# Halving a group's last hidden chunk earlier, finishing only the sums a norm needs, and GpSimd's low halves in two instructions, in a two-block fp32 network

## The chip, the cores and the metric

One NeuronCore of a Trainium2 chip runs the whole network in one launch. The metric is the device time of one execution in microseconds (us); lower is better. The kernel is bound to one core, so its own span is the time, but for some 2 us around it.

## The reference, cut to what matters

Two blocks run one after the other on 256 tokens of width 1024, all in fp32. The first block has two layers with a 256-token context stream beside the latent one; every norm in it is modulated by a vector (shift, scale, gate) that is itself a product of a conditioning vector with a 1024 x 6144 matrix.

```python
mod = split(silu(c) @ w_mod[i] + b_mod[i], 6)          # sh1, sc1, ga1, sh2, sc2, ga2
...
h = rmsnorm(x, g_pre_mix) * (1 + sc1) + sh1
u = h @ w_in                                            # four mixers, then w_out
...
x = x + ga1 * rmsnorm(y, g_post_mix)
hm = rmsnorm(x, g_pre_mlp) * (1 + sc2) + sh2
x = x + ga2 * rmsnorm(square(relu(hm @ w_mlp1)) @ w_mlp2, g_post_mlp)
```

In the first layer the context rows pass through the same MLP (hidden width 4096), so that MLP works on 512 tokens; this wide MLP is where the first part of the change lies. The second block is an attention block with a gated convolutional feed-forward of hidden width 2816.

## The kernel before, in words

**Three matmuls for one.** Every fp32 product is made of three float32r matmuls (`mm3`, lines 430 to 432): high by high, low by high, high by low. So every weight is split into a high half H (ACT, a copy that rounds) and a low half L (raw minus H).

**Weight units.** The weights come as a list of 128 x 1024 units in the order of their use. `fetch` brings two units (1 MB) per DMA from SP into one of four `raw` buffers. `step` splits the next unit: H by ACT (line 373), L by line 375, a subtraction of two SBUF operands, on DVE for 197 units and on POOL for 117, as the place in the program decides. Last-minute units are split in two halves of 512 columns into other buffers (`uH` line 366, `uL` line 367, POOL). Six H and six L buffers exist. `take(lead)` hands out the next unit and first sees to it that units up to `lead` places further on are split (`pump`): the lead thus sets where the H and L instructions stand in the program order of ACT and DVE.

**Modulation.** The list also holds units of the modulation matrix ("mod" units), spread over the program, two at a time. `mods` takes them: they aren't split; DVE (lines 692, 696), or ACT with POOL (lines 688, 690), scales each by the conditioning vector and adds it to an accumulator `macc`, 128 x 512, twice per unit. When a vector is whole, PE sums over partitions (`mod`, line 706), DVE adds the bias (`mr`, line 710) and, for a gate, the post-norm's gain (line 657); later steps that turn the row into columns (`modT`, PE line 770, DVE copy line 775) or into a split gate row (`mrh`, ACT lines 665 and 666, DVE line 667) are put in a list, `later`, and done where `run_later` is called.

**The wide MLP** (`mlp_wide`) has nine steps, g = 0 to 8. Step g makes four hidden chunks of 128 hidden rows by 512 tokens (`m1`, 24 matmuls of 512 columns for each, in one PSUM bank), then multiplies the four chunks of step g-1 with four `m2` units into 4 x 2 output tiles (96 matmuls), which DVE adds to `yacc`. `hidden` turns a chunk into its squared relu, split: ACT `rl` (line 1807) and `hidH` (1813), DVE `m` (1814) and `hidL` (1815), which is the last reader of the chunk's PSUM bank. Two mod units stand after chunk 1 and after chunk 3 of a step and two more pairs among the products. At chunk 3 the four m2 units are taken with leads 3, 2, 1, 0, and taking the first of them does the two mod units that stand ahead of it. The first output tile pair (`first[0]`, `first[1]`) is computed with chunks 0 to 2 first (9 matmuls each) and chunk 3 after. At g = 6 PE also makes the rows of a gate (`gaT`, line 812), which ACT (line 818) and DVE (line 816) copy out of PSUM as `ga`.

**From layer 0 to layer 1.** During step 8 the output tiles are finished row block by row block: post norm, `gp` (line 948), new `X` (line 962), statistics, `xn` (line 846). Then PE transposes `xn` (`hT`, line 886), DVE and ACT make `hF`, `hH`, `hL` (lines 870, 874, 875) with the modulation columns that `affine` hands out, and the first product of layer 1 (`ag`) starts. `affine` empties the whole `later` list first.

**Where GpSimd's subtractions stand.** Most of the 117 POOL subtractions come in bursts of 2 to 6 at the norms between stages, and three per step in the feed-forward at the end of the program (1345 to 1454 us).

Of the kernel before, what the change touches and what calls it, by code (L numbers as in the profile page):

```python
# [16 lines left out]
ALU = mybir.AluOpType  # L17
# [35 lines left out]
M1_MODS = ((0, 0, 0, 0), (0, 0, 0, 2), (0, 2, 0, 2), (0, 2, 0, 2)) + ((0, 2, 0, 2),) * 4  # L53
# [250 lines left out]
class Program:  # L304
# [45 lines left out]
    def step(self, pool=False, k2=False):  # L350

        nc = self.nc
        self.fetch()
        m = self.entries[self.next_entry][1]
        t = self.raw[self.next_entry]
        j = self.part
        self.n += 1
        if self.unit_names[len(self.units)][0] == "mod":
            self.units.append((t[:, j, :], self.next_entry))
            self.waiting[self.next_entry] = self.waiting.get(self.next_entry, 0) + 1  # L360
        elif k2:
            u = []
            for i in range(2):
                hi, lo = self.k2("uH", dt=F32R), self.k2("uL", dt=F32R)
                src = t[:, j, 512 * i:512 * i + 512]
                nc.scalar.activation(hi, src, AF.Copy)  # L366
                nc.gpsimd.tensor_tensor(lo, src, hi, op=ALU.subtract)  # L367
                u.append((hi, lo))
            self.units.append(u)
        else:  # L370
            hi = self.splitp.tile([128, 1024], F32R, tag="H", name=f"H_{self.n}")
            lo = self.splitp.tile([128, 1024], F32R, tag="L", name=f"L_{self.n}")
            nc.scalar.activation(hi, t[:, j, :], AF.Copy)  # L373
            pool = pool or (self.pool_l and len(self.units) % self.pool_l == 0)
            (nc.gpsimd if pool else nc.vector).tensor_tensor(lo, t[:, j, :], hi, op=ALU.subtract)  # L375
            self.units.append((hi, lo))
        self.part = (j + 1) % m
        t = None
        if self.part == 0:
            del self.raw[self.next_entry]  # L380
            if self.next_entry in self.waiting:
                self.held.add(self.next_entry)
            self.next_entry += 1
            self.fetch()

    def pump(self, upto, pool=(), k2=False):

        pool = list(pool)
        while len(self.units) <= upto and self.next_entry < len(self.entries):
            if len(self.units) > self.used and len(self.held) > RAW_BUFS - 2 and self.unit_names[len(self.units)][0] == "mod":  # L390
                break
            self.step(pool.pop(0) if pool else False, k2)
# [392 lines left out]

    def affine(self, l, which, i):

        self.run_later(True)
        return self.modT[l, 3 * which + 1][:, i], self.modT[l, 3 * which][:, i]

    def bcast_row(self, i, half):
# [1026 lines left out]
    def mlp_wide(self, l, hs, ctx_part, gates):  # L1818

        nc, v = self.nc, self.nc.vector  # L1820
        yacc, hids, h = {}, {}, hs[0]

        def product(ps, hid, us, t, hf, j):
            a = tuple(z[:, 128 * t:128 * t + 128] for z in hid[j])
            b = tuple(z[:, 512 * hf:512 * hf + 512] for z in us[j])
            self.mm3(ps, a, b, j == 0, j == 3)

        for g in range(9):
            if g < 8:
                hids.setdefault(g, [])  # L1830
                if g == 1:
                    self.pool_l = MLP_POOL
                if g == 0:
                    us = [self.unit("m1", lead=max(3 - j, 0)) for j in range(6)]
                    bk = [self.ps("m1") for _ in range(6)]
                    for j in range(0, 6, 2):
                        self.chunks(us[j:j + 2], h, 0, 256, bk[j:j + 2])
                    ctx_part(lambda k0: k0 and self.chunks(us[:2], h, 256, 512, bk[:2], range(k0 - 2, k0)))
                    self.chunks(us[:2], h, 256, 512, bk[:2], range(6, 8))
                    hids[1] = []  # L1840
                    for j in range(6):
                        if j > 1:
                            self.chunk(us[j], h, [(256, 512)], bk[j])
                        us[j] = None
                        self.hidden(bk[j], 512, hids[j // 4])
                        bk[j] = None
                        self.pump(self.used + j)
                else:
                    for j in range(len(hids[g]), 4):
                        ps = self.flat_chunk("m1", h, [(0, 512)])  # L1850
                        if j == 1 and g > 3:
                            self.mods(2, 0)
                        if j == 3:
                            us = [self.unit("m2", lead=3 - j) for j in range(4)]
                        self.hidden(ps, 512, hids[g])
            if g == 7:
                self.pool_l = False
                h = None
                hs.clear()
            if g == ROPE_AT[0]:  # L1860
                self.rope_tables()
            if g == ROPE_AT[1]:
                self.rope_rows()
                self.lam_value()
            if g == 6:
                gates()
            if g > 0:
                if g == 8:
                    us = [self.unit("m2", lead=3 - j) for j in range(4)]
                    self.pump(self.used + 1)  # L1870
                hid = hids.pop(g - 1)
                first = [self.ps("m2") for _ in range(2)] if g < 8 else ()
                for t in range(4):
                    for hf in range(2):
                        ps = first[hf] if t == 0 and first else self.ps("m2")
                        js = range(4)
                        if t == 0 and first:
                            js = (3,)
                            if hf == 0:
                                for i in range(2):  # L1880
                                    for j in range(3):
                                        product(first[i], hid, us, 0, i, j)
                        for j in js:
                            if g == 8 and t == 3 and hf == 1 and j == 2:
                                us[:2] = None, None
                                yield None
                            product(ps, hid, us, t, hf, j)
                        if hf and t == 0:
                            first = ()
                        if g < 8 and 2 * t + hf in M2_PUMP:  # L1890
                            self.pump(self.used + M2_PUMP[2 * t + hf] + (g == 7))
                        if g == 1:
                            yacc[t, hf] = self.k2("yacc")
                            nc.scalar.activation(yacc[t, hf], ps, AF.Copy)
                        elif g < 8:
                            v.tensor_tensor(yacc[t, hf], ps, yacc[t, hf], op=ALU.add)
                        if g < 8:
                            self.mods(M2_MODS[g][2 * t + hf], 0)
                        else:
                            yield ps, yacc.pop((t, hf))  # L1900

    def ffn_narrow(self, step, downs, name, nj, ga, xn=None):


# [7 lines left out]
        for i, ds in enumerate(downs):  # L1912
            if i == len(downs) - FFN_OFF:
                self.pool_l = False
            if xn is None and i == len(downs) - 1:
                self.pump(self.used + END_H)
                self.pump(self.used + 8, k2=True)
            hid.update(step(i))
            for c in ds:
                if not acc:  # L1920
                    acc = [[self.ps("acc") for _ in range(2)] for _ in range(2)]
                u = self.unit(name)
                for t in range(2):
                    for hf in range(2):
                        down(c, u, t, hf)
                u = None
                del hid[c]
# [24 lines left out]
    def block1(self, l, h):  # L1952
# [58 lines left out]
        for _ in self.ffn_narrow(step, MLP_DOWN, "m2", 32, ga, out):  # L2011
            h = None
            pairs += self.new_pairs()
            self.pre_tile(out[0], self.pk("pre_mix_2", 0, 8), None, pairs, 0)
# [509 lines left out]
```

## Time and profile before

| what | value |
|---|---|
| median of 3 runs (lowest to highest) | 1493.54 us (1491.67 to 1496.65) |
| the profiled execution's own time | 1495.41 us |
| its span, first to last instruction | 1493.2 us |
| busy: PE, PEld | 1428.6 us (96%), 1194.3 us |
| busy: DVE, ACT, POOL | 941.1, 768.4, 544.0 us |
| mean granted TensorE clock | 0.987 |

The busy shares are of the span. PE is busy nearly always, so what can be had is in PE's waits and in the stretches where its clock was granted at half. A row of the timeline shows the start, the length and, in brackets, the idle time just before and what ended it. A 512-column matmul is drawn 0.39 us long but the next one starts 0.22 to 0.23 us after it, since matmuls are pipelined.

### The profile page before, as it was taken

How to read it: one execution, taken by the hardware profiler on the slowest of the kernel's cores; microseconds unless marked ns; L12 is line 12 of the kernel's file. 1: busy time of each engine (PE TensorE's matmuls, PEld its weight loads, DVE VectorE, ACT ScalarE, POOL GpSimd, SP SyncE). 2: the span in 40 equal slices, each digit the busy share in tenths (PEclk: the TensorE clock that was granted, in tenths of full speed). 3: DMA queues.
4: the chain of work that ended last, by engine and by line, in shares of the span. 5: the costliest groups of instructions: out<-in, count | busy, mean ns of one | idle time of the engine just before them, and what ended most of it. 6: DMA issues, size and time to landing. Idle time of an engine off the chain costs nothing.

```text
span 1493.2 us, 21581 instructions
## 1 busy us (share of the span) xinstructions
PE 1428.6 (96%) x8260; PEld 1194.3 (80%) x8260; DVE 941.1 (63%) x1642; ACT 768.4 (51%) x1406; POOL 544.0 (36%) x351
## 2 busy tenths in 40 slices
PE   8989999999999998998899899998999999999998
PEld 7766767888778787877777689996888899789997
DVE  4685573765866676788776765556466666754335
ACT  4446564555553323345666554455434664556554
POOL 2384531203551500007263500005022555738882
PEclk9999999999999999998999999999999999999999
DMA  9653631124554553634242455555555433545551
GB/s 342 211 199 142 140 110 69 60 83 165 178 194 160 191 204 130 220 146 149 87 84 93 142 187 180 187 180 189 180 188 190 138 122 113 203 148 186 177 190 57
DMA packets 73103, 235.71 MB, mean 158 GB/s; under 512 B 13536, under 2 KB 14248, under 8 KB 73000
## 3 DMA queue, kind: packets, MB, share of 16 engines
q1 hardware_dynamic: 72280, 233.65, 46.3%
q8 instruction: 65, 1.06, 0.3%
q10 hardware_dynamic: 720, 0.69, 0.1%
q14 instruction: 38, 0.31, 0.1%
HBM read 233.27 MB, written 1.05 MB: 157 GB/s over the span
## 4 chain that ended last, share of the span: by engine, by line
PE 72%; DVE 16%; ACT 8%; issue 2%; DMA 1%; SPq 0%; DVEq 0%; ACTq 0%
PE m L431 8%; PE m L432 8%; PE m L430 8%; PE acc L430 3%; PE acc L431 3%; PE acc L432 3%; DVE L L375 3%; PE pj L431 2%; PE pj L430 2%; PE pj L432 2%; PE up L430 2%; PE up L432 2%; PE up L431 2%; ACT H L373 2%; ACT P L1447 1%
## 5 line engine op out<-in xcount | busy, mean ns | idle before, releaser
L375 POOL TENSOR_TENSOR L<-raw,H 128x1024 fp32r<-128x1024 f32 x117 | 283.3, 2443 | 323.0 <-ACT H L373 305.6
L373 ACT ACTIVATE H<-raw 128x1024 fp32r<-128x1024 f32 x314 | 317.3, 1050 | 131.4 <-PE m L432 48.1
L375 DVE TENSOR_TENSOR L<-raw,H 128x1024 fp32r<-128x1024 f32 x197 | 254.6, 1321 | 90.4 <-ACT H L373 87.8
L367 POOL TENSOR_TENSOR uL<-raw,uH 128x512 fp32r<-128x512 f32 x32 | 46.1, 1472 | 192.1 <-ACT uH L366 192.1
L431 PE MATMUL m<-hL,H 128*128 128x512 f32 (+1 forms) x304 | 109.0, 358 | 2.0 <-DVE hL L875 2.0
L430 PE MATMUL m<-hH,H 128*128 128x512 f32 (+1 forms) x304 | 109.0, 358 | 1.0 <-ACT hH L874 1.0
L432 PE MATMUL m<-hH,L 128*128 128x512 f32 (+1 forms) x304 | 108.7, 358 | 1.2 <-DVE L L375 1.2
L431 PE MATMUL m<-L,hidH 128*128 128x512 f32 x256 | 101.7, 397 | 4.2 <-DVE L L375 4.2
L1807 ACT ACTIVATE rl<-m 128x512 f32<-128x512 f32 (+1 forms) x56 | 28.3, 505 | 150.3 <-PE m L432 150.1
L430 PE MATMUL m<-H,hidH 128*128 128x512 f32 x256 | 101.7, 397 | 3.9 <-DVE hidL L1815 3.9
L432 PE MATMUL m<-H,hidL 128*128 128x512 f32 x256 | 100.7, 393 | 0.0
L690 POOL TENSOR_TENSOR macc<-mt,macc 128x512 f32<-128x512 f32 x42 | 61.1, 1494 | 92.3 <-ACT mt L688 92.3
L1026 POOL TENSOR_TENSOR cfacc<-cft,cfacc 128x512 f32<-128x512 f32 (+1 forms) x60 | 64.6, 1077 | 54.7 <-ACT cft L1025 50.8
L430 PE MATMUL up<-h,H 128*128 128x256 f32 x288 | 81.8, 284 | 0.0
L432 PE MATMUL up<-h,L 128*128 128x256 f32 x288 | 81.5, 283 | 0.0
L431 PE MATMUL up<-h,H 128*128 128x256 f32 x288 | 81.5, 283 | 0.0
L1814 DVE TENSOR_TENSOR m<-m,rl 128x512 f32<-128x512 f32 (+1 forms) x56 | 32.7, 584 | 76.6 <-ACT rl L1807 76.4
L696 DVE SCALAR_TENSOR_TENSOR macc<-raw,csil,macc 128x512 f32<-128x512 f32 x98 | 66.9, 749 | 0.0
L431 PEld LDWEIGHTS m<-hL,H 128*128 128x128 f32 x304 | 57.7, 190 | 10.9 <-DVE hL L875 2.6
L432 PEld LDWEIGHTS m<-hH,L 128*128 128x128 f32 x304 | 57.8, 190 | 10.1 <-DVE L L375 2.0
L430 PEld LDWEIGHTS m<-hH,H 128*128 128x128 f32 x304 | 57.9, 190 | 9.2 <-ACT hH L874 1.2
L2099 POOL TENSOR_TENSOR ra<-ra,rb 128x512 f32<-128x512 f32 x16 | 21.6, 1351 | 113.8 <-DVE rb L2097 113.3
(547 smaller groups left out, 4060.5 us busy)
## 6 DMA issues: line engine op xcount, KB each, us to landing
raw<-in_wst SPq DMA_DIRECT2D x208, 1024.0 KB
mod<-in_wmod SPq DMA_DIRECT2D x16, 256.0 KB
X<-in_x SPq DMA_DIRECT2D x4, 512.0 KB
nab<-in_rpb SPq DMA_DIRECT2D x32, 64.0 KB
raw<-in_wst SPq DMA_DIRECT2D x2, 512.0 KB
wuq<-in_small SPq DMA_DIRECT2D x4, 256.0 KB
cst<-in_c SPq DMA_DIRECT2D x4, 256.0 KB
grow<-in_rows SPq DMA_DIRECT2D x4, 256.0 KB
```

The lines of the kernel that those rows point to most:

```text
L367: nc.gpsimd.tensor_tensor(lo, src, hi, op=ALU.subtract)
L373: nc.scalar.activation(hi, t[:, j, :], AF.Copy)
L375: (nc.gpsimd if pool else nc.vector).tensor_tensor(lo, t[:, j, :], hi, op=ALU.subtract)
L430: mm(out, a[0], b[0], start=start, stop=False)
L431: mm(out, a[0], b[1], start=False, stop=False)
L432: mm(out, a[1], b[0], start=False, stop=stop)
L690: nc.gpsimd.tensor_tensor(o, t, o, op=ALU.add)
L696: v.scalar_tensor_tensor(acc[i][j], a, c, o, op0=ALU.mult, op1=ALU.add)
L1026: nc.gpsimd.tensor_tensor(acc, t, acc, op=ALU.add)
L1807: nc.scalar.activation(r[:, :T], ps[:, :T], AF.Relu)
L1814: v.tensor_tensor(ps[:, :T], ps[:, :T], r[:, :T], op=ALU.mult)
L2099: self.nc.gpsimd.tensor_tensor(a, a, b, op=ALU.add)
```

## The change

Three edits, and nothing else:

1. In `mlp_wide`, chunk 3 of a step is taken with a lead that reaches over the two mod units to the fourth m2 unit (4 + 2 = 6 places where two mod units follow, 4 where none does), so that all m2 units are split before the mod units are worked on; and `hidden` is called for a chunk right behind its matmuls, before the mod units instead of behind them.
2. `affine` does `later` steps only until the two column sets that it hands out exist; the rest is done at a new call in step 8 of the wide MLP, ahead of the products of the second row block, or where `run_later` is called next.
3. `low_half` makes the L of a unit: on POOL as two subtractions of 128 x 512, on DVE as one of 128 x 1024 as before. A reader of the first 512 columns waits for the first of the two alone.

```diff
@@ step
-            (nc.gpsimd if pool else nc.vector).tensor_tensor(lo, t[:, j, :], hi, op=ALU.subtract)
+            self.low_half(lo, t[:, j, :], hi, pool)
...
+    def low_half(self, lo, src, hi, pool):
+
+        e, n = (self.nc.gpsimd, 512) if pool else (self.nc.vector, 1024)
+        for o in range(0, 1024, n):
+            e.tensor_tensor(lo[:, o:o + n], src[:, o:o + n], hi[:, o:o + n], op=ALU.subtract)
...
@@ affine
-        self.run_later(True)
+        while any((l, 3 * which + j) not in self.modT for j in range(2)):
+            self.later.pop(0)[1]()
...
@@ mlp_wide
-                        ps = self.flat_chunk("m1", h, [(0, 512)])
+                        ps = self.flat_chunk("m1", h, [(0, 512)], 4 + M1_MODS[g][3] if j == 3 else None)
+                        self.hidden(ps, 512, hids[g])
                         if j == 1 and g > 3:
                             self.mods(2, 0)
                         if j == 3:
                             us = [self.unit("m2", lead=3 - j) for j in range(4)]
-                        self.hidden(ps, 512, hids[g])
...
+                        if g == 8 and t == 1 and hf == 0:
+                            self.run_later()
```

How the instructions move is seen best in the order of each engine. On DVE, at the end of step g = 6 of the wide MLP (L is the low half of a weight unit, `mr` a finished modulation row, `macc` the work on two mod units, `m` and `hidL` chunk 3's hidden values), it stood before:

```order
L375 TENSOR_TENSOR L_5240<-raw_5114,H_5239 128x1024
L710 TENSOR_TENSOR mr_4_5275<-mod_5270,brow 128x256
L375 TENSOR_TENSOR L_5278<-raw_5161,H_5277 128x1024
L692 TENSOR_SCALAR macc_5283<-raw_5077,csil 128x512
L692 TENSOR_SCALAR macc_5284<-raw_5077,csil 128x512
L375 TENSOR_TENSOR L_5288<-raw_5161,H_5287 128x1024
L696 SCALAR_TENSOR_TENSOR macc_5283<-raw_5077,csil,macc_5283 128x512
L696 SCALAR_TENSOR_TENSOR macc_5284<-raw_5077,csil,macc_5284 128x512
L1814 TENSOR_TENSOR m_1049_5245<-m_1049_5245,rl_5297 128x512
L1815 TENSOR_TENSOR hidL_5300<-m_1049_5245,hidH_5299 128x512
```

and with the change:

```order
L390 TENSOR_TENSOR L_5259<-raw_5133,H_5258 128x1024
L390 TENSOR_TENSOR L_5265<-raw_5180,H_5264 128x1024
L390 TENSOR_TENSOR L_5269<-raw_5180,H_5268 128x1024
L716 TENSOR_TENSOR mr_4_5304<-mod_5299,brow 128x256
L1821 TENSOR_TENSOR m_1052_5274<-m_1052_5274,rl_5306 128x512
L1822 TENSOR_TENSOR hidL_5309<-m_1052_5274,hidH_5308 128x512
L698 TENSOR_SCALAR macc_5315<-raw_5096,csil 128x512
L698 TENSOR_SCALAR macc_5316<-raw_5096,csil 128x512
L702 SCALAR_TENSOR_TENSOR macc_5315<-raw_5096,csil,macc_5315 128x512
L702 SCALAR_TENSOR_TENSOR macc_5316<-raw_5096,csil,macc_5316 128x512
```

Two L moved ahead of `mr`, and `m` and `hidL` ahead of four `macc`; the other steps from 2 on have the same pattern, on ACT the third H and `rl`, `hidH` move ahead of its own `macc` work likewise.

On PE, at the passage from layer 0 to layer 1 (m is the last output tile of the MLP, hT the transposes of layer 1's normalised rows), it stood before:

```order
L432 MATMUL m_1199_6024<-H_5800,hidL_5568 128x512
L770 MATMUL modT_6047<-ident,mr_3_5644 128x128 x2
L706 MATMUL mod_6053<-macc_5777,pick 32x256 x2
L706 MATMUL mod_6053<-macc_5779,pick 32x256 x2
L886 MATMUL hT_6065<-ident,xn_5906 128x128
```

and with the change the three rows stand some 66 matmuls earlier, at the start of the second row block's products:

```order
L438 MATMUL m_1157_5879<-H_5844,hidL_5678 128x512
L776 MATMUL modT_5930<-ident,mr_3_5673 128x128 x2
L712 MATMUL mod_5936<-macc_5796,pick 32x256 x2
L712 MATMUL mod_5936<-macc_5798,pick 32x256 x2
L436 MATMUL m_1173_5929<-H_5815,hidH_5540 128x512
```

Their DVE work (`modT` copies, `mr` twice) moves with them, and the DVE step `mrh` of the same vector moves from ahead of the first `hF` to later in layer 1.

On POOL the instructions keep their order; each L becomes a pair, here the first three (cfacc is the depthwise convolution), before:

```order
L375 TENSOR_TENSOR L_1474<-raw_1362,H_1473 128x1024
L1026 TENSOR_TENSOR cfacc_903<-cft_1488,cfacc_903 128x512
L1026 TENSOR_TENSOR cfacc_903<-cft_1491,cfacc_903 128x512
L1026 TENSOR_TENSOR cfacc_903<-cft_1494,cfacc_903 128x512
L375 TENSOR_TENSOR L_1552<-raw_1483,H_1551 128x1024
L375 TENSOR_TENSOR L_1562<-raw_1483,H_1561 128x1024
```

and with the change:

```order
L390 TENSOR_TENSOR L_1474<-raw_1362,H_1473 128x512 x2
L1033 TENSOR_TENSOR cfacc_903<-cft_1489,cfacc_903 128x512
L1033 TENSOR_TENSOR cfacc_903<-cft_1492,cfacc_903 128x512
L1033 TENSOR_TENSOR cfacc_903<-cft_1495,cfacc_903 128x512
L390 TENSOR_TENSOR L_1553<-raw_1484,H_1552 128x512 x2
L390 TENSOR_TENSOR L_1564<-raw_1484,H_1563 128x512 x2
```

Only the shape and the count of the L rows changed.

## Rows read from the trace of the kernel before

**Rows 1.** The page: busy time of each engine; the chain that ended last.

```profile
PE 1428.6 (96%) x8260; PEld 1194.3 (80%) x8260; DVE 941.1 (63%) x1642; ACT 768.4 (51%) x1406; POOL 544.0 (36%) x351
...
PE 72%; DVE 16%; ACT 8%; issue 2%; DMA 1%; SPq 0%; DVEq 0%; ACTq 0%
```

**Rows 2.** Waits of PE, whole span: waited for, us in total, times, longest.

```profile
PE m L431 <- DVE L L375: 4.2, 7, 1.6
PE ab L432 <- DVE h L912: 4.1, 5, 0.9
...
PE tok L431 <- POOL L L375: 2.5, 2, 1.8
```

**Rows 3.** Timeline of DVE, end of step 2's chunks.

```profile
383.26 0.42 DVE L710 TENSOR_TENSOR mr<-mod,brow 128x256 f32<-128x256 f32 x1 [2.45 <-PE mod L706]
...
384.20 2.30 DVE L375 TENSOR_TENSOR L<-raw,H 128x1024 fp32r<-128x1024 f32 x1
```

**Rows 4.** Waits of PE in 384 to 392, 430 to 438, 520 to 528.

```profile
PE m L431 <- DVE L L375: 2.1, 2, 1.6
...
PE m L431 <- DVE L L375: 0.7, 2, 0.5
...
PE m L431 <- DVE L L375: 0.3, 1, 0.3
```

**Rows 5.** Timeline of DVE, end of step 6's chunks.

```profile
567.83 0.42 DVE L710 TENSOR_TENSOR mr<-mod,brow 128x256 f32<-128x256 f32 x1 [2.57 <-PE mod L706]
568.16 1.22 DVE L375 TENSOR_TENSOR L<-raw,H 128x1024 fp32r<-128x1024 f32 x1
...
573.33 0.69 DVE L1814 TENSOR_TENSOR m<-m,rl 128x512 f32<-128x512 f32 x1
574.12 0.69 DVE L1815 TENSOR_TENSOR hidL<-m,hidH 128x512 fp32r<-128x512 f32 x1
```

**Rows 6.** Timeline of PE, first products of step 6.

```profile
570.37 0.39 PE L431 MATMUL m<-L,hidH 128*128 128x512 f32 x1
570.59 0.39 PE L432 MATMUL m<-H,hidL 128*128 128x512 f32 x1
574.87 0.79 PE L430 MATMUL m<-H,hidH 128*128 128x512 f32 x1 [3.89 <-DVE hidL L1815]
```

**Rows 7.** Windows: busy (instructions) by engine, PEclk, DMA share, GB/s.

```profile
574.00:580.00 6.00, 5.13 (x12) 4.07 (x13) 2.50 (x10) 3.18 (x5) 0.08 (x1) 0.50 0.86 334
```

**Rows 8.** Timeline of ACT, step 6.

```profile
562.96 2.94 ACT L373 ACTIVATE H<-raw 128x1024 fp32r<-128x1024 f32 x3
...
575.24 1.07 ACT L818 ACTIVATE ga<-gaT 128x512 f32<-128x512 f32 x2
```

**Rows 9.** Timeline of PE, passage from layer 0 to layer 1.

```profile
664.58 0.64 PE L706 MATMUL mod<-macc,pick 128*32 128x256 f32 x8
...
669.92 0.39 PE L430 MATMUL ag<-hH,H 128*128 128x256 f32 x1 [1.11 <-ACT hH L874]
```

**Rows 10.** Timeline of DVE, the same passage.

```profile
668.48 0.48 DVE L667 SCALAR_TENSOR_TENSOR mrh<-mrh,low,mr 128x256 fp32r<-128x256 f32 x1 [1.03 <-ACT mr L666]
```

**Rows 11.** Timeline of POOL: last feed-forward, last units, then three bursts at norms.

```profile
1394.37 7.15 POOL L375 TENSOR_TENSOR L<-raw,H 128x1024 fp32r<-128x1024 f32 x3 [1.35 <-ACT H L373]
...
1464.77 8.44 POOL L367 TENSOR_TENSOR uL<-raw,uH 128x512 fp32r<-128x512 f32 x6 [8.49 <-ACT uH L366]
...
284.00 4.90 POOL L375 TENSOR_TENSOR L<-raw,H 128x1024 fp32r<-128x1024 f32 x2 [30.42 <-ACT H L373]
...
835.46 10.16 POOL L375 TENSOR_TENSOR L<-raw,H 128x1024 fp32r<-128x1024 f32 x4
...
1345.22 14.23 POOL L375 TENSOR_TENSOR L<-raw,H 128x1024 fp32r<-128x1024 f32 x6 [4.16 <-ACT H L373]
```

**Rows 12.** DVE during the burst at 835; line 912: duration ns min/median/max.

```profile
838.56 4.81 DVE L912 TENSOR_TENSOR h<-hF,h 128x256 fp32r<-128x256 f32 x2
...
L912 DVE TENSOR_TENSOR h<-hF,h x24: 409/426/2602, 835.0 to 1311.0; 128x256 fp32r<-128x256 f32 x24
```

## The prediction

> **What bounds the kernel now.** I read the page first. PE is busy 96% of the span, and 72% of the chain of waits is PE [rows 1]; so a change that takes no matmul away can only win what PE waits for, and what its clock loses behind a wait. The waits of PE come next: a long list of short ones, of which three groups bear on the change, DVE's L (4.2 us), DVE's h (4.1) and POOL's L (2.5) [rows 2]; hidL stands apart, with one wait of 3.89 [rows 6]. Then the timeline around each, to see what the late instruction had stood behind. In [rows 3] DVE first sits idle for 2.45 us, held at `mr` by PE's `mod`, and then does an L in 2.30 us instead of the 1.22 of [rows 5]: work that could have filled the idle time is queued behind the instruction that waits. In [rows 5] the same idle time is 2.57, and `m` and `hidL` come at the end of the queue.
>
> A wait costs a little more than its idle time. Matmuls are drawn 0.39 us long but start 0.22 apart [rows 6], some 0.23 when averaged; a stall hides the difference of 0.16, so I add that for each.
>
> **Part 1, the wide MLP.** Nothing is added or removed; instructions change places.
>
> Steps 2, 3 and 5: PE waits for the L of the third and fourth m2 units, 2.1 + 0.7 + 0.3 us in five waits [rows 4]; with 5 x 0.16 that is 3.9. After the change both L stand ahead of `mr`, in the 2.45 us in which DVE idles [rows 3], and two of them need 2 x 1.22 = 2.44 there if their H is ready. The ACT order puts the third H directly behind the second, so I take the whole 3.9. If a `raw` buffer arrives late or ACT does, part of it stays: bounds 1.5 to 3.9.
>
> Step 6: PE stops at 570.59 and goes on at 574.87 because `first[1]` was given the PSUM bank that `hidL` reads last, and `hidL` ends at 574.12 + 0.69 [rows 5, 6]. The loss is 4.28 - 0.23 = 4.05. Behind the stall PE's clock is granted at 0.50, that is 1.2 of 2.4 GHz: from 574.87 to 580 it does 12 matmuls [rows 7] in 5.1 us that at 0.23 would take 2.8, so 2.3 more. After the change three H are ready (they already run back to back from 562.96 [rows 8]), both L fit into the 2.57 of idle time, and behind `mr` at 567.83 come `m` and `hidL` at once: 567.83 + 0.42 + 2 x 0.75 = 569.8, ahead of 570.8, when PE wants the bank. So the stall goes, and with it the half clock: 6.3. What is late next is `ga`: PE reaches the second row of output tiles some 24 matmuls (5.5 us) behind 568.75, at 574.2, and two of those banks hold `gaT` until ACT's 1.07 us copies at 575.24 are through [rows 8]. These follow a small DVE chain (`pr`) that stood last on DVE and still does; its start moves from 574.8 to about 569.8 + 4 x 0.66 = 572.4, so the copies end near 573.9. Just in time; this is the weak point of the term. Bounds 2 to 6.3.
>
> The four `macc` that now come later (by two L and two short steps) are read a whole vector later; nobody waits for them. One raw DMA moves ahead of the bias rows' DMAs on SP's queue early in the MLP; its 1 MB is wanted sooner than they are, and I cost that at nothing.
>
> Term 1: -(3.9 + 6.3) = -10.2, between -3.5 and -10.2.
>
> **Part 2, the sums a norm needs.** At the passage PE does `modT` and `mod` (the latter 0.64 us [rows 9]) ahead of the transposes, and DVE's `hF` stands behind `mrh`, which itself idles 1.03 for ACT [rows 10]; PE then waits 1.11 for ACT's hH [rows 9]. With `mrh` gone from there, `hF` can start when the transposes are in, a good microsecond sooner. PE's own `modT` and `mod` aren't saved, only done earlier, beside nothing: they still cost PE what they did. The moved DVE steps (two `mr` of 0.42 [rows 5] and two small copies, some 1.1 us) now stand ahead of the second row block, where DVE has to keep up. So the gain is at most the 1.11 (with 0.16, 1.3), at least nothing, or a loss of 1.1 if DVE's steps come through to `xn`. I take -1.0, since the wait ends on ACT and DVE work that the change makes shorter.
>
> **Part 3, halves on POOL.** No row of before shows a 128 x 512 L in a burst. Three whole ones take 7.15 us, 2.38 each; the nearest row is `uL`, the same subtraction on 512 columns, six in 8.44, so 1.41 each [rows 11]. Half of 2.38, 1.19, is the lower bound, 1.41 the upper (each `uL` may also have waited for its H); I take 1.3, nearer to the middle. A unit then costs 2.6 instead of 2.38, and 117 units 26 us of POOL. In the feed-forward at the end POOL does three L and then idles 1.35 [rows 11], and so nine times running; three units cost 0.7 more, which the idle time covers. At 1.41 it is 1.3, and still covered, barely.
>
> What it gives: [rows 12] show `h` at 409 ns at its shortest, and two of them taking 4.81 us while POOL runs four L in 10.16 instead of 9.5 [rows 11]. So a DVE instruction with two SBUF operands waits for POOL's instruction to end and goes before the next. With halves such a wait is half as long, some 1.2 us less each time, and PE's 4.1 us behind `h` [rows 2] shrink; a reader of the first half goes on 1.3 sooner, which bears on the 2.5 behind POOL's L. Against that a burst of four ends 0.9 later, and as more DVE steps get in between, later still; the row sums of the norm behind it inherit that. Bounds: all 6.6 us and some clock behind them won, -9; or a loss at the nine bursts beside norms (2 units at 284 us, 4 at 835, 6 at 1345 [rows 11], 27 in all): 0.25 for each unit, +7. I take -2: half of the 4.1, and the rest given back.
>
> The Trainium skill (GPSIMD Engine Reference, section 8, Key points) says that GpSimd shares its SBUF interfaces with VectorE, in contention with instructions that have two SBUF inputs. The trace agrees as to which instructions suffer (`h`, 2602 ns at the longest for 409). The page does not say that the loser waits for a whole instruction; were it a sharing in proportion, term 3 would be a loss alone.
>
> **The sum.** 1495.4 (the profiled execution's own time) - 10.2 - 1.0 - 2.0 = 1482.2. That execution lies 1.9 above the median of the runs, so 1480.3 on the median's level; I say **1480**. All times below are on that level.
>
> **The rivals.**
>
> A. *The MLP's stalls only change hands.* In step 6 `ga` or the clock's drop takes over what `hidL` held up, and in steps 2 and 3 the third H is late. For: the `ga` copies come within 0.3 us of PE. Against: three H are early in step 6. Term 1 is then -3.5 and the rest as before: 1487.
>
> B. *The norms win in full.* All waits behind `h` and POOL's L go, the clock holds there, and term 3 is -9: 1473. Against: behind each such wait stands a chain of small DVE steps that is as long as before.
>
> C. *Contention is in proportion.* POOL and DVE slow each other whatever the length of an instruction: halves win nothing, and the 0.22 per unit is paid where PE waits on a burst, 27 x 0.22 / 2 = +3: 1493.5 - 10.2 - 1.0 + 3 = 1485. Against: the waits of `h` are multiples of POOL's rest, not stretched evenly. This is what the skill's sentence, read by itself, would suggest.
>
> D. *POOL becomes the bound: slower.* A half costs more than `uL` shows, because DVE steps in at every boundary. With h us per half, nine periods of the last feed-forward, 8.5 us each (7.15 + 1.35), become 6h, and half of what 27 units in bursts lose comes through: 9 x (6h - 8.5) + 13.5 x (2h - 2.38). At h = 1.48 that is 3.4 + 7.8 = 11.2, all that terms 1 and 2 bring; this is the point that decides. At 1.6 it is 9.9 + 11.1 = 21, and the time 1493.5 - 11.2 + 21 = 1503. For: 1.41 is near. Against: in that stage the three L take 7.15 without a disturbance, and a half with the same work per column has no reason to cost 35% more.
>
> E. *It does not do what it says.* The lead of 6 reaches the third and fourth m2 units, but their raw data isn't there, and DVE, standing at that L, holds `mr` and `hidL` up as before; term 1 is nothing, term 3 a loss of 1 to 2: 1493.5, no change.
>
> **How the numbers follow.** Forecast 0.55, A 0.17, B 0.09, C 0.08, D 0.07, E 0.04. A measurement of this kernel can tell about 0.3% (4.5 us) from no change. Faster by more than that: the forecast, B, C, and most of A, 0.83; with a little taken off for the bounds of the terms, 0.81. Within: E, the rest of A and the edge of D, 0.12. Slower: 0.07. The range takes in the forecast with its bounds, A, C and most of B: 1470 to 1489; D, E and the far end of B are left out, under 0.2.
>
> **What would show it.** Step by step in the profile of the changed kernel: no wait of PE on DVE's L or hidL in the wide MLP (4.2 and 3.9 go to under 1), full clock at 574 to 580 (moved on by what was won before), two L in DVE's idle time ahead of `mr`; PE's wait at `ag` under 0.3; L on POOL as 234 instructions of 1.2 to 1.4 us, POOL busy near 570, DVE's `h` never above 1.8 us. I am wrong if PE's waits at step 6 only carry another name (`ga`), if POOL's halves take 1.48 or more, or if the time is above 1489.

## The result, and the profile after

The changed kernel takes 1479.18 us (median of 4 runs, 1478.29 to 1479.58), against 1494.81 for the kernel before in the same comparison: a ratio of 0.9888, 95% interval 0.9872 to 0.9905. The forecast was 1480 with a range of 1470 to 1489.

The page of the changed kernel (busy time, share of the span, instructions; then the chain of waits, and POOL's L with its idle time):

```profile
span 1477.5 us, 21712 instructions
...
PE 1423.5 (96%) x8260; PEld 1192.8 (81%) x8260; DVE 929.6 (63%) x1642; ACT 767.3 (52%) x1406; POOL 560.9 (38%) x468
...
PE 75%; DVE 13%; ACT 8%; issue 3%; DMA 1%; SPq 0%; DVEq 0%; ACTq 0%
...
L390 POOL TENSOR_TENSOR L<-raw,H 128x512 fp32r<-128x512 f32 x234 | 307.3, 1346 | 295.7 <-ACT H L373 279.7
```

Against [rows 1], 3 points of DVE's share of the chain have gone over to PE, and POOL is busy 17 us longer. The waits of PE (waited for, us in total, times, longest), where [rows 2] stood:

```profile
PE hT L926 <- DVE xn L853: 9.7, 7, 2.2
PE tok L437 <- POOL L L390: 2.9, 3, 1.3
PE S L1471 <- ACT P L1454: 2.4, 1, 2.4
...
PE ab L437 <- POOL L L390: 2.0, 4, 0.7
...
PE m L437 <- DVE L L390: 1.2, 2, 0.8
```

(`ab` is the first product of a narrow feed-forward, `tok` a product of the mixers, `S` attention scores.) DVE's `h` and `hidL` are no longer in the list, and the L that `m` waited for 4.2 us is down to 1.2. The head of the list, `xn`, has grown to 9.7 us. It was the head before as well, which [rows 2] don't show:

```profile
PE hT L919 <- DVE xn L846: 5.5, 5, 2.5
```

**Step 6 of the wide MLP.** The timeline of DVE, in the place of [rows 5]:

```profile
554.93 3.50 DVE L390 TENSOR_TENSOR L<-raw,H 128x1024 fp32r<-128x1024 f32 x3
558.73 0.42 DVE L716 TENSOR_TENSOR mr<-mod,brow 128x256 f32<-128x256 f32 x1 [0.30 <-PE mod L712]
559.07 0.69 DVE L1821 TENSOR_TENSOR m<-m,rl 128x512 f32<-128x512 f32 x1
559.86 0.69 DVE L1822 TENSOR_TENSOR hidL<-m,hidH 128x512 fp32r<-128x512 f32 x1
```

Three L run in a row, DVE's idle time ahead of `mr` is 0.30 us instead of 2.57, and `hidL` follows at once. The windows of the same kernel (columns as in [rows 7]) and ACT's copies of `ga`:

```profile
558.00:570.00 12.00, 12.00 (x63) 9.79 (x63) 11.08 (x23) 7.49 (x11) 2.65 (x8) 1.00 0.66 258
```

```profile
563.70 1.06 ACT L825 ACTIVATE ga<-gaT 128x512 f32<-128x512 f32 x2
```

PE doesn't stop and keeps its full clock, where 574 to 580 had 0.50. `ga` is ready at 564.8; the first 24 matmuls began at 559.65 and take until 565.1. So the weak point held, by 0.3 us.

**Where the time went.** I laid the traces against each other: the start of each matmul in one less the start of the same matmul in the other. The table gives, for stretches on the span of before, by how many us each kernel gains (-) or loses (+) there; e1 to e4 and e7 are experiments told below.

| stretch of before, us | changed kernel | e1: part 1 alone | e2: part 2 alone | e3: part 3 alone | e4: parts 1, 2 | e7: quarters |
|---|---|---|---|---|---|---|
| 0 to 270 | -0.1 | +2.6 | -1.0 | +0.7 | +2.8 | -4.4 |
| 270 to 329 (norm) | -3.2 | -1.6 | 0.0 | -3.2 | 0.0 | -4.0 |
| 329 to 639 (wide MLP) | -12.8 | -12.8 | -0.2 | -1.1 | -12.5 | -11.2 |
| 639 to 695 (passage) | -4.9 | -0.1 | -1.6 | -3.3 | -1.5 | -5.0 |
| 695 to 829 (mixers) | +1.0 | -1.8 | -1.3 | -0.9 | +0.7 | -5.4 |
| 829 to 859 (norm) | +2.4 | 0.0 | 0.0 | +0.6 | 0.0 | -0.9 |
| 859 to 1051 | +0.8 | +0.5 | -0.2 | -0.5 | -0.2 | -2.8 |
| 1051 to 1488 | +1.0 | 0.0 | 0.0 | +0.7 | +0.3 | -0.2 |

One execution has its own jitter: 0 to 270 moves by 3 to 4 us between kernels that are equal there (e1, e2, e4), and 270 to 329 and 695 to 829 give part 1 alone -1.6 and -1.8 although nothing of it stands there. The MLP's row is steadier: -12.5 to -12.8 in the changed kernel, e1 and e4, 1.6 less in e7 at one wait near 490 us that e9, e11 and e12 don't have.

**The norms.** At the passage PE goes into `ag` without the 1.11 us of [rows 9]. At the norm ahead of layer 1's narrow MLP DVE's `h` are short, and the steps behind them long. The timeline of DVE in the changed kernel:

```profile
816.06 1.19 DVE L919 TENSOR_TENSOR h<-hF,h 128x256 fp32r<-128x256 f32 x1
...
817.49 2.63 DVE L919 TENSOR_TENSOR h<-hF,h 128x256 fp32r<-128x256 f32 x2
...
823.82 3.44 DVE L969 SCALAR_TENSOR_TENSOR X<-gp,rs_y,X 128x512 f32<-128x512 f32 x2
```

of POOL:

```profile
815.50 11.21 POOL L390 TENSOR_TENSOR L<-raw,H 128x512 fp32r<-128x512 f32 x8
```

of PE, and the windows behind it:

```profile
829.71 1.26 PE L926 MATMUL hT<-ident,xn 128*128 128x128 f32 x8 [2.22 <-DVE xn L853]
```

```profile
832.00:838.00 6.00, 6.00 (x16) 4.65 (x16) 4.09 (x7) 3.15 (x6) 0.00 (x0) 0.55 0.07 5
```

The two `h` of [rows 12] take 2.63 instead of 4.81, and PE's three stalls there, 2.9 us together, are gone. These were, in the kernel before (`sse` is the small step on DVE behind the last `h`):

```profile
PE ab L432 <- DVE h L912: 1.6, 2, 0.9
PE ab L432 <- DVE sse L855: 0.9, 1, 0.9
```

But POOL's burst ends at 826.7, and X, two DVE instructions with two SBUF operands, now falls into it and takes 3.44. Before, X came after the burst:

```profile
846.05 1.42 DVE L962 SCALAR_TENSOR_TENSOR X<-gp,rs_y,X 128x512 f32<-128x512 f32 x2
```

PE waits 2.22 for `xn`, and behind that one long wait its clock is at half. Before, 2.9 us were lost in three pieces with idle times under 0.9 us, and the clock held (1.00 from 843 to 857). The half clock makes the difference: +2.4 in the table.

### The profile page after: what moved, and what is told of

It is laid out like the page before. It is cut to its first block, busy times and chain, and to the rows that moved or that the text cites. A ratio compares the mean times of both kernels' runs of the same rounds, so it can differ in the third digit from the quotient of the medians.

```text
span 1477.5 us, 21712 instructions
## 1 busy us (share of the span) xinstructions
PE 1423.5 (96%) x8260; PEld 1192.8 (81%) x8260; DVE 929.6 (63%) x1642; ACT 767.3 (52%) x1406; POOL 560.9 (38%) x468
## 4 chain that ended last, share of the span: by engine, by line
PE 75%; DVE 13%; ACT 8%; issue 3%; DMA 1%; SPq 0%; DVEq 0%; ACTq 0%
PE m L436 9%; PE m L437 9%; PE m L438 9%; PE acc L437 3%; PE acc L436 3%; PE acc L438 3%; PE pj L438 2%; PE pj L437 2%; PE pj L436 2%; PE up L436 2%; PE up L438 2%; PE up L437 2%; ACT H L373 2%; DVE L L390 1%; DVE X L969 1%
## 5 line engine op out<-in xcount | busy, mean ns | idle before, releaser
L390 POOL TENSOR_TENSOR L<-raw,H 128x512 fp32r<-128x512 f32 x234 | 307.3, 1346 | 295.7 <-ACT H L373 279.7
L390 DVE TENSOR_TENSOR L<-raw,H 128x1024 fp32r<-128x1024 f32 x197 | 247.0, 1287 | 94.3 <-ACT H L373 92.3
L696 POOL TENSOR_TENSOR macc<-mt,macc 128x512 f32<-128x512 f32 x42 | 56.9, 1385 | 98.4 <-ACT mt L694 86.7
```

Of the source, the lines that this page charges most:

```text
L390: e.tensor_tensor(lo[:, o:o + n], src[:, o:o + n], hi[:, o:o + n], op=ALU.subtract)
L696: nc.gpsimd.tensor_tensor(o, t, o, op=ALU.add)
```

## The experiments

Each kernel was timed in 3 rounds against the kernel before on the same chip; ratios have their 95% interval. The expectations count 340 to 640 us on the trace's own clock, which starts 11 us before the span; it is the MLP's row of the table.

**e1, part 1 alone.** The edit is the MLP's hunk of the change on the kernel before.

> Part 1 alone (lead over the mod units, hidden values ahead of them). Theory: the gain of the changed kernel is mostly the wide MLP's, and POOL's subtractions have no share in it, since POOL makes no L there. Laid against each other matmul by matmul, the two traces part by 12.7 us between 340 and 640 us; so this kernel should be 12 to 13 us below before, some 1482, with no wait on hidL and no half clock at step 6. Rival: the MLP's gain needs the other parts (ACT or DVE late from the norms ahead of it), and alone it gives under 8 us.

Measured: 1482.85 us, ratio 0.9907 (0.9888 to 0.9927), -12.8 us in the MLP's row, no wait on `hidL`. The theory stands: the gain in the MLP needs neither of the other parts.

**e2, part 2 alone.**

> Part 2 alone (affine finishes only what it hands out). Theory: the wait of PE at the first ag (1.11 us on ACT hH) shrinks to a few tenths or goes, and PE's modT and mod are paid earlier; net -1 us, 0 to -1.5, which the time cannot show and the trace can. Rival: the moved DVE steps come through to xn, and the transposes start later by up to 1.1: net 0 or a loss.

Measured: 1492.86 us, ratio 0.9985 (0.9974 to 0.9996). In the trace PE pays +0.9 at the start of the second row block, gets it back ahead of the transposes, and saves 1.3 + 0.3 at the first `ag`: -1.6 from 639 to 695. The moved DVE steps do not come through to `xn`. The waits of PE at `ag`, before and in e2:

```profile
PE ag L430 <- ACT hH L874: 1.1, 1, 1.1
```

```profile
PE ag L430 <- ACT hH L875: 0.5, 1, 0.5
```

The 0.5 is a later `ag`, not the first.

**e3, part 3 alone.** The edit is `low_half` on the kernel before.

> Part 3 alone (POOL's L in two instructions). Theory: DVE instructions with two SBUF operands wait for the end of POOL's instruction, so the longest h falls from 2.6 to about 1.3 us, at all norms, and PE's waits behind h go; but as more DVE steps meet a boundary, the later steps (X, the row sums) meet POOL too, and at the two bursts of four the wait for xn takes back what h gave: the sum is -2 us, between -5 and +2, so no change that the time can tell. Rival 1: contention is in proportion, h keeps its 2.6 us, loss of 1 to 3. Rival 2: POOL time is the bound, the last feed-forward longer by 5 us or more.

Measured: 1488.94 us, ratio 0.9958 (0.9943 to 0.9973): a gain of 4 to 8.5 us by the times, more than expected, 7.0 in the one trace. Most of it lies at the norm from 270 to 329 and at the passage. Part of it is the clock: leaving out the first 60 us and the end, it was at half for 20 us in this trace and for 31 before, and at half clock half of such time is lost. The waits of PE ahead of the narrow MLP show the swap by itself, without the other parts:

```profile
PE hT L925 <- DVE xn L852: 2.2, 1, 2.2
PE ab L437 <- POOL L L390: 0.4, 1, 0.4
PE ab L436 <- ACT h L917: 0.3, 1, 0.3
```

**e4, parts 1 and 2 without the halves.**

> Parts 1 and 2 without part 3. Theory: the parts add, so this is before less 13 to 14.5 us, some 1481, within 3 us of the changed kernel. Rival: the halves carry a share of more than 4 us, and this kernel is at 1484 or above; or they cost, and it is below 1477.

Measured: 1483.18 us, ratio 0.9912 (0.9897 to 0.9927). This is 4.0 us above the changed kernel by the medians, past the theory's 3 and just short of the rival's 1484. On top of the other two parts the halves bring 3.6 us by the ratios, with their two intervals 0 to 7, and some 2.3 in the traces behind 270 us. That is less than alone by every one of these numbers, but the intervals overlap, so it isn't shown by the times. In the traces the clock bears on it: with the halves it was at half for 31 us, without them (e4) for 27, and the same wait of 2.22 us for `xn` has 6.8 us of half clock behind it in the changed kernel and 3.4 in e3.

**e5, only the lead**, and **e6, only the earlier call of `hidden`**:

```diff
-                        ps = self.flat_chunk("m1", h, [(0, 512)])
+                        ps = self.flat_chunk("m1", h, [(0, 512)], 4 + M1_MODS[g][3] if j == 3 else None)
```

```diff
                         ps = self.flat_chunk("m1", h, [(0, 512)])
+                        self.hidden(ps, 512, hids[g])
...
-                        self.hidden(ps, 512, hids[g])
```

> Only the lead of part 1: both L move ahead of mr, but m and hidL stay behind the four macc. Theory: two late instructions make the MLP's waits, and each edit cures one of them. The waits on L (4.9 us between 340 and 560 with the MLP change) go, and hidL comes two L earlier, at about 572.3 on the time of before, so the wait at step 6 falls from 4.05 to some 1.6 and the half clock behind it may go too: 8 to 11 us below before of the 12.8 that the trace of part 1 alone has in the MLP. Rival: only the place of hidL counts, and this gives under 5.

> Only the call of hidden ahead of the mod units: m and hidL come before four macc and two L. Theory: the wait on hidL at step 6 goes, but the two L come 1.5 us later in every step, so the waits on L grow in steps 2 to 7 by up to 1.5 each: 4 us better to 3 worse than before, far from the 12.8 of both. Rival: the L have room, and this gives 6 or more.

Measured: e5 1483.26 us, ratio 0.9927 (0.9909 to 0.9945), -11.2 in the MLP, just over the 8 to 11 expected; one wait is left at step 6:

```profile
PE m L430 <- DVE hidL L1815: 1.3, 1, 1.3
```

e6 1498.31 us, ratio 1.0024 (1.0012 to 1.0037), +2.0 in the MLP; over 340 to 660 us its waits of PE are

```profile
PE m L431 <- DVE L L375: 9.4, 10, 1.8
```

So the two edits belong together in one way only: the lead does most by itself, the earlier `hidden` takes the rest, and alone it pushes the L back and loses. (It does cure step 6, -5.2 there, and gives it all up in the other steps.)

**e7, quarters.** POOL's L in four instructions of 256 columns, on the changed kernel:

```diff
-        e, n = (self.nc.gpsimd, 512) if pool else (self.nc.vector, 1024)
+        e, n = (self.nc.gpsimd, 256) if pool else (self.nc.vector, 1024)
```

> The changed kernel with POOL's L in four instructions of 256 columns. Theory (a two-operand DVE instruction waits for the end of POOL's one): the longest h falls again, from 1.3 to some 0.8 us; a unit costs POOL about 2.9 us instead of 2.6, three of them 8.8 in the last feed-forward, more than its 8.5 a period, and DVE's X chain at the bursts of four meets POOL for longer: 0 to 6 us slower than the changed kernel. Rival (contention in proportion): h unchanged against halves.

Measured: 1461.81 us (1460.06 to 1462.74), ratio to before 0.9779 (0.9762 to 0.9797). That is 17 us below the changed kernel (16 by the ratios), where I expected it to be no faster. The waits of PE in this kernel:

```profile
PE ab L437 <- POOL L L390: 6.0, 10, 0.9
PE hT L926 <- DVE xn L853: 3.2, 5, 0.8
PE tok L437 <- POOL L L390: 2.9, 3, 1.5
```

DVE at the same norm, POOL's burst there, and the windows of the norm and behind it:

```profile
806.85 1.52 DVE L919 TENSOR_TENSOR h<-hF,h 128x256 fp32r<-128x256 f32 x2
...
811.80 2.34 DVE L969 SCALAR_TENSOR_TENSOR X<-gp,rs_y,X 128x512 f32<-128x512 f32 x2
```

```profile
805.40 13.13 POOL L390 TENSOR_TENSOR L<-raw,H 128x256 fp32r<-128x256 f32 x16
```

```profile
815.00:819.00 4.00, 2.33 (x8) 1.34 (x9) 3.14 (x6) 0.97 (x3) 3.53 (x5) 1.00 0.25 102
819.00:826.00 7.00, 6.24 (x32) 4.97 (x31) 5.05 (x10) 4.74 (x10) 0.00 (x0) 1.00 0.47 150
```

The burst is longer still, 13.13 us. But `h` and X meet shorter instructions, POOL is late to PE by three pieces of 0.4 to 0.8 us, `xn` by 0.8 at the most, and the clock stays at 1.00. Leaving out the first 60 us and the end, the clock was at half for 31 us in the changed kernel, as long as before though at other places, and for 10 us with quarters; at half clock half of such time is lost, so up to 10 of the 18 us between the two traces are the clock, and the rest waits. (4 of the 18 lie ahead of 270 us, where e9 and e11, quarters too, have -0.1 and -0.2: jitter.)

The longest `h`, which I expected at 0.8, is 1.48:

```profile
L919 DVE TENSOR_TENSOR h<-hF,h x24: 407/426/1483, 804.9 to 1277.0; 128x256 fp32r<-128x256 f32 x24
```

It meets a `uL` of 128 x 512, which this edit doesn't touch. The three `h` that meet L at this norm take 2.29, 2.29 and 2.60 us with whole L, 1.19, 1.19 and 1.52 with halves, 0.63, 0.64 and 0.89 with quarters; the longest over a `uL` takes 1.47 to 1.49 in all three. So it isn't that `h` is unchanged, as the rival had it. In the last feed-forward POOL has no idle time left, as I had feared, and nobody waits for it:

```profile
1311.28 111.71 POOL L390 TENSOR_TENSOR L<-raw,H 128x256 fp32r<-128x256 f32 x160 [2.77 <-ACT H L373]
```

**e8, two L of each burst of four on DVE**, on the changed kernel:

```diff
                         us[4 - first:6 - first] = None, None
-                        self.pump(self.used + 7, pool=ALL)
+                        self.pump(self.used + 7)
```

> The changed kernel, but the last two L of each of the two bursts of four (ahead of the narrow feed-forwards) on DVE. Theory: there POOL's burst ends before DVE's row sums and X, which then take 1.4 instead of 3.4 us; two L cost DVE 2.5 in the same chain; the wait of PE for xn falls from 2.2 us to about 1 or less, and the half clock behind it (2.3 us, each time) goes: 2 to 6 us below the changed kernel, 1473 to 1477. Rival: the chain is as long with two L in it, and the time is that of the changed kernel, or longer.

Measured: 1474.09 us (1471.68 to 1480.41), ratio 0.9867 (0.9831 to 0.9902), an interval that overlaps the changed kernel's. DVE, and the waits of PE at that norm:

```profile
820.61 3.44 DVE L390 TENSOR_TENSOR L<-raw,H 128x1024 fp32r<-128x1024 f32 x2
...
825.58 1.42 DVE L969 SCALAR_TENSOR_TENSOR X<-gp,rs_y,X 128x512 f32<-128x512 f32 x2
```

```profile
PE hT L926 <- DVE xn L853: 3.6, 3, 2.1
```

X takes 1.42 us again, as the theory had it, but the two L take 3.44 in the same chain and PE waits 2.1 us for `xn`, about as long as in the changed kernel. The rival was right about the wait; the time lies where the theory had it, but what the trace gains there (2.0 us) is a shorter stretch at half clock.

**e9, the same with quarters.**

> Quarters, with the last two L of each burst of four on DVE. With quarters PE's waits at those bursts were on POOL's L (1.8 us ahead of the feed-forward of layer 1) and on xn (1.5). Theory: POOL's burst is now the late one there, so moving half of it to DVE takes these waits, 1 to 4 us below quarters, 1458 to 1461. Rival: DVE's two L stand in the chain to xn and cost what POOL's wait did: within 1 us of quarters, or slower.

Measured: 1460.59 us, ratio 0.9763 (0.9748 to 0.9777), an interval that overlaps that of quarters. PE's waits on POOL's L for `ab` fall from 6.0 to 2.9 us, and the two norms gain 1.4 us each in the trace; the time cannot tell it from quarters.

```profile
PE ab L437 <- POOL L L390: 2.9, 6, 0.9
```

**e10, eighths** (`128` for `256`):

> L on POOL in eight instructions of 128 columns. From the medians 2.41, 2 x 1.30 and 4 x 0.742 each further instruction costs 0.187 us, so a unit would take 3.7. Theory: the grain has won what it can with quarters (half clock only at one norm, no wait on h), and POOL, which with quarters ran 160 instructions without a gap in the last feed-forward and just kept up, becomes the bound there: 40 units at 3.7 are 149 us where PE needs about 112 for them, so PE waits on POOL's L and the kernel is 20 to 40 us slower than quarters, 1480 to 1500. Rival: the stage has slack, and eighths are within 3 us of quarters.

Measured: 1500.86 us, ratio 1.0034 (1.0016 to 1.0051), 39 us above quarters. POOL in the last feed-forward, then the waits of PE:

```profile
1335.20 139.28 POOL L390 TENSOR_TENSOR L<-raw,H 128x128 fp32r<-128x128 f32 x320 [0.47 <-ACT H L373]
```

```profile
PE acc L437 <- POOL L L390: 12.7, 21, 1.7
PE ab L437 <- POOL L L390: 9.0, 13, 1.1
PE o L437 <- DVE L L390: 6.1, 1, 6.1
```

POOL is the bound there: against quarters 22.7 us are lost behind 1319 us. The 139 us for 40 units are a little under the 149 expected. But the other half of the loss, +12 ahead of the last norm and +7 in layer 1's mixers, is another thing: DVE's L, held up for many of POOL's instructions. Line 390 on DVE (duration ns min/median/max), and one such place, first on DVE, then on POOL:

```profile
L390 DVE TENSOR_TENSOR L<-raw,H x197: 1208/1224/9810, 19.6 to 1472.8; 128x1024 fp32r<-128x1024 f32 x197
```

```profile
1250.58 14.90 DVE L390 TENSOR_TENSOR L<-raw,H 128x1024 fp32r<-128x1024 f32 x2 [1.47 <-ACT H L373]
```

```profile
1232.40 24.62 POOL L390 TENSOR_TENSOR L<-raw,H 128x128 fp32r<-128x128 f32 x56 [0.36 <-PE mx L437]
1256.99 6.19 POOL L367 TENSOR_TENSOR uL<-raw,uH 128x512 fp32r<-128x512 f32 x5
```

The first of the two L takes 6.13 us, over eighths; the second 8.84 us, nearly all of it over `uL`, six in a row of which the view has five.

**e11, quarters, with whole L in the last feed-forward.**

> Quarters everywhere but in the last feed-forward, where POOL's 46 L are whole again. Theory: all that quarters win lies at the norms and mixers, where two-operand DVE steps meet POOL's bursts, and POOL's fullness in the last feed-forward cost nothing: within 1.5 us of quarters (1460 to 1463), POOL busy 25 us less. Rival: the fine grain helps DVE's steps there too, and this is 3 us or more slower; or POOL's fullness did cost, and it is faster by as much.

Measured: 1463.72 us, ratio 0.9779 (0.9759 to 0.98), the ratio of quarters; in the trace not a tenth of a us differs from 1051 us on, and POOL is busy 574.1 us instead of 598.0. So nothing that quarters win is won in the last feed-forward, and POOL at full load there cost nothing.

**e12, quarters written from the last to the first.**

```diff
-        for o in range(0, 1024, n):
+        for o in reversed(range(0, 1024, n)):
```

> Quarters, written from the last to the first, so that the reader of an L, who begins with the first columns, waits for all four, as for a whole L; the grain that DVE meets on POOL is that of quarters. Theory: quarters win by DVE's shorter waits and by the clock that holds behind them, so this keeps at least half of the 17 us that quarters are below halves; the early start of readers is lost, up to 2.2 us at each of some six bursts: 3 to 9 us above quarters, 1465 to 1471. Rival: the early start of the readers is what quarters win, and this is back at the halves' time, 1477 or above.

Measured: 1463.83 us, ratio 0.9788 (0.9771 to 0.9804), only 2 us above quarters by the medians, less than expected, and with an interval that overlaps that of quarters. The waits of PE on POOL's L grow as they must, those on `xn` don't:

```profile
PE ab L437 <- POOL L L390: 8.8, 7, 1.6
PE tok L437 <- POOL L L390: 4.3, 3, 2.3
...
PE hT L926 <- DVE xn L853: 2.7, 4, 0.8
```

So the early start of PE on the first columns is worth 2 of the 17 us or so; the time cannot tell it from nothing. What is left for the rest is what DVE meets on POOL, and that is the same as with quarters (the sum of DVE's lost time, explained below, is 47 us in both).

## Why the prediction was right, point by point

**The sum.** The gain forecast was 13.2 us; by the medians of the same comparison it was 15.6. That the time came within 1 us of 1480 is in part luck: the kernel before was at 1494.81 in that comparison, 1.3 above the level that the forecast started from.

**Part 1, -10.2 predicted, -12.5 to -12.8 measured.** Steps 2, 3 and 5 came as worked out: in the matmuls, -1.78 and -0.63, -0.37 and -0.63, -0.49, together 3.9. Step 6 gave 6.8 instead of 6.3, the stall of 4.05 and the half clock. The term was too small by what I had not listed: 0.9 at a wait of hidden chunk 1 on its L near 500 us, which the earlier place of L and `hidden` cures too, and some 1.2 in pieces too small for the list of waits. One sign failed: PE's waits on L in this MLP were to go under 1 us, and 1.2 and 0.4 are left there. e5 and e6 show that the reason was the right one, late L behind `mr`, and `hidL` behind both; rivals A and E are out.

**Part 2, -1.0 predicted, -1.6 measured** (e2), just over the bound of 1.3 that I gave. The wait of 1.11 went, and the `ag` behind it came 0.3 closer together.

**Part 3, -2.0 predicted; 3.6 us less on top of the other parts** (e4, 0 to 7 with the intervals). The price was a little high: a half is drawn 1297 ns long at the median, the 1.3 that I took, but they overlap by some 0.05. POOL's timeline in the last feed-forward of the changed kernel, where [rows 11] had three in 7.15 and 1.35 of idle time:

```profile
1387.10 7.57 POOL L390 TENSOR_TENSOR L<-raw,H 128x512 fp32r<-128x512 f32 x6 [0.94 <-ACT H L373]
```

That is 0.14 for a unit instead of 0.22, and POOL's busy time rose by 17 us instead of 26. The course was as told: the waits behind `h` went, and "the rest given back" was given back, by X and `xn`. The waits for `xn`, the largest group in PE's list before, were not among those that the prediction looked at. What I sized at nothing is the clock: "some clock behind them" stood only in the bound, and at two norms (829 and 1291 us on the span of before) the halves traded three short waits for one long one and a half clock. In the other direction e3 alone wins more than 2, by the times 4 or more; rival B's 9 in full it doesn't reach. Rival C (contention in proportion) is out: the longest `h` is 2602 ns with whole L, 1520 with halves.

```profile
L919 DVE TENSOR_TENSOR h<-hF,h x24: 409/426/1520, 815.0 to 1293.9; 128x256 fp32r<-128x256 f32 x24
```

The Trainium skill says this outright on a page that I had not weighed (SBUF — State Buffer, the section on SBUF's two separate sides): the pair of ports that DVE and GpSimd share is an exclusive lock, held for the whole instruction, and the loser fully blocks. These traces agree nearly always (the 76 of 77 below), and not with eighths.

**Rival D named a real mechanism and had the wrong sum for it.** Quarters take 2.79 us a unit (111.71 / 40), as halves of 1.40 would: by my formula they would lose nothing in the last feed-forward, where three of them in 8.4 just fit the period of 8.5, and 13.5 x (2.79 - 2.38) = 5.5 us at the norms. The first came true, and at the norms they won instead: the formula counted what POOL spends and left out what DVE gets back. With eighths, 3.48 us a unit (139.28 / 40), three take 10.4, and there POOL is the bound, as D said.

How much DVE loses, summed over its instructions that take over 0.25 us more than the median of their kind (same line, tiles and shape): 81 us before, 64 in the changed kernel, 47 with quarters, 58 with eighths. The optimum of the four sizes is quarters, and the change stopped short of it: quarters beat both kernels, at 0.9779 of before against 0.9888.

## What to carry to other kernels

Where an engine idles at an instruction that waits for another engine, look at what is queued behind it and could have run: moving two weight splits and one activation there, without touching the work, gave most of this gain. When two engines hold each other up, the length of one instruction is what the other mostly waits, so cut the long one until its fixed cost per piece outweighs the shorter waits, and try the next size up and down rather than reason to the point. And look at the longest piece of a stall: at the two norms here three waits under 0.9 us cost their own length, and one of 2.2 cost the clock behind it as well. That isn't certain for every wait of this length: behind the 2.4 us that PE waited for `S` in the changed kernel the clock stayed at 1.00.

## What the runs showed of the hardware that I had not expected

Cutting costs POOL the same for each piece. In the last feed-forward, where they run in a row, whole units start 2.37 us apart, halves 1.25, quarters 0.70 and eighths 0.42 (medians): 2.37, 2.50, 2.79 and 3.36 for a unit, 0.14 us for each instruction added.

A blocked DVE instruction does not always get in at the next boundary. Of the 77 blocked ones before (those of the sum above), 76 lie over a single POOL instruction and one over two. With quarters 76 of 83 lie over one, and one L is held over two whole ones and parts of two others (3.25 us). With eighths five of 56 were held over 5 to 20 whole ones, four of them L, the longest for 9.81 us. There POOL's eighths start 0.42 us apart and are drawn 0.46 long, so there is no gap between them. But the size alone does not decide: the L of 8.84 us was held over `uL` of 128 x 512, which also follow each other without a gap, and which in the kernel before hold a DVE instruction for one of them at a time. Why a run of POOL instructions sometimes holds DVE off over many of them wasn't tried, and stays open.
